# A seven-product matrix multiply: scaled fp16 and five products by quarters, against unscaled fp16 and six

## The chip, the cores and the metric

The kernel runs on one core of one Trainium2 chip. The metric is the device time of one execution in microseconds (us). Lower is better. Below, PE is the matrix engine, DVE the vector engine, ACT the scalar engine, POOL the GpSimd engine, and SP the engine whose queue issues every DMA here. SBUF is the on-chip memory of 128 partitions, PSUM the accumulators that matmuls write: eight banks of 128x512 float32.

## The reference

```python
B, S, D = 8, 2048, 2048
x = np.random.randn(B, S, D).astype(np.float32)
w = np.random.randn(D, D).astype(np.float32)

def reference(x, w):
    cs = np.cumsum(x, axis=1)
    diff = cs - (cs shifted by one row, first row zero)
    return np.matmul(diff, w).astype(np.float32)
```

The difference of a running sum is the input again, so what has to be computed is a product of a 16384x2048 matrix with a 2048x2048 matrix.

## The kernel before

**Tiles.** x is cut into 128 tiles of 128 rows. Tiles 0 to 3 are multiplied plainly while w is still arriving. The other 124 go in 31 groups of four tiles, called g, h = g+2, and their partners g+1 and h+1. One group is a block product: the left matrix has the quarters A11, A12 (tiles g and h, left and right half of the inner dimension) and A21, A22 (the partners), and w has the quarters B11, B12, B21, B22 of 1024x1024. Each group forms the result by Winograd's seven products instead of eight: P1 = A11 B11, P2 = A12 B21, P3 = S4 B22, P4 = A22 T4, P5 = S1 T1, S2 T2 and S3 T3. The sums S1 to S4 are made for every group, by DVE, from transposed x tiles in fp16. The sums T1 to T4 are made of w, once.

**Products and quarters.** A product taken whole costs 32 matmuls of 128x128 by 128x512 (line 532, `matmuls`). A product "by quarters" applies the same seven-product scheme once more inside itself, on quarters of 512: it costs 28 matmuls (line 554, `quarter`). It needs four sums of x pieces (128x512 fp16), and sums Q1 to Q4 of quarters of T or B (128x2048 fp16). In the class `Quarters` the seven steps are called slots:

```python
        def slot(self, i):
            h, g, b = self.h, self.g, self.right.b
            to, left, right, start = (
                (h[0], "a11", "t11", True),
                (h[1], "s1", "Q1", True),
                (h[0], "s2", "Q2", False),
                (g[0], "a12", "t21", False),
                (h[0], "s3", "Q3", False),
                (g[1], "s4", "t22", False),
                (h[0], "a22", "Q4", False),
            )[i]
            quarter(f"{self.name}.{i}", to, getattr(self, left), b[right], start)
            if i == 0:
                copy(f"{self.name}.first", g[0], h[0])
            elif i in (2, 4):
                copy(f"{self.name}.out{i}", self.lent, h[0])
```

The three copies are ACT's (line 571). With them go two DVE additions, `middle` and `last`, of a PSUM bank and a copy in SBUF (line 520). Sum s3 is POOL's, the other three are DVE's (line 520 too).

From the third group on, P1 to P5 go by quarters and S2 T2 and S3 T3 whole: 5 x 28 + 2 x 32 = 204 matmuls. The first group takes all seven whole (224), the second takes P2 and P3 by quarters (216).

Some Q sums stay in SBUF. Six are made anew in each group by DVE (`give`), into one buffer `flow` which every one of them shares. One more is brought back from DRAM (`bring`, 512 KB).

**Scaling.** x and w are scaled before the conversion to fp16: w by its largest magnitude (line 291, while it arrives, and line 415), each x tile by the mean of its absolute values. For a tile, ACT sums magnitudes (`weigh`, line 138), POOL and DVE make the scale and its reciprocal (lines 157, 159, 160), ACT converts (`narrow`, line 170), and two transposing DMAs bring the halves into the layout that PE needs (`turn`, line 186). Results are scaled back where they leave PSUM: `keep` copies a bank with a factor (ACT, line 568), and `add` adds a bank times a factor to what was kept (DVE, SCALAR_TENSOR_TENSOR, line 579). There are 20 of these additions in a group. Two finished results of a group go to DRAM for each pair of tiles, in 512 KB pieces (`put`).

**Order.** Every operation is recorded with a label. A table `places` written out by hand gives each label a position for the prelude, for single groups and (`None`) for all others; each engine issues its operations in that order and waits only by semaphores. So the engines' queues are fixed, and an operation that waits holds up all that stands behind it on its engine.

Of the kernel before, what the change touches and what calls it, by code (L numbers as in the profile page):

```python
# [10 lines left out]
def kernel(  # L11
# [17 lines left out]
    bf16 = mybir.dt.bfloat16  # L29
    f32 = mybir.dt.float32  # L30
    ADD = mybir.AluOpType.add
    SUB = mybir.AluOpType.subtract
    MUL = mybir.AluOpType.mult
    MAX = mybir.AluOpType.max
    AX = mybir.AxisListType
    COPY = mybir.ActivationFunctionType.Copy
    ABS = mybir.ActivationFunctionType.Abs
    TOP = 2048.0
    ROW = 4000.0
    TINY = 1e-34  # L40
# [4 lines left out]
    PERIOD = 2168  # L45
# [7 lines left out]
    W = [Wall[:, k, :] for k in range(KH)]  # L53
    whole = [t.rearrange("p (a h n) -> p a h n", a=2, h=2) for t in W]
    pieces = [
        t.bitcast(f16).rearrange("p (i n j c) -> p i j n c", i=4, j=2, c=NB) for t in W
    ]
    B11, T1, B12, T2, B21, T3, B22, T4 = (
        [p[:, i // 2, i % 2] for p in pieces] for i in range(8)
    )  # L60
    fours = Wall.bitcast(f16).rearrange("p k (i n j c) -> p k i j n c", i=4, j=2, c=NB)
    tiny = const.tile([P, 64], f32, name="tiny")
    sums_at = [tiny[:, ds(2 * i, 2)] for i in range(4)]
    means_at = [tiny[:, ds(i, 1)] for i in (8, 9, 13, 14)]
    uw, uinv, wred = (tiny[:, ds(10 + i, 1)] for i in range(3))
    scales_at = [tiny[:, ds(16 + i, 1)] for i in range(8)]
    units_at = [tiny[:, ds(24 + i, 1)] for i in range(8)]
    wmax = tiny[:, ds(32, 2 * KO)]
    waste = const.tile([P, NH], mybir.dt.uint8, name="waste")
    eye = waste[:, : 2 * P].bitcast(bf16)  # L70
    F = const.tile([P, 4, NH], f32, name="F")
    turned_x = [
        [const.tile([P, KH, P], f16, name=f"x{i}{j}") for j in range(2)] for i in range(4)
    ]

    arena = const.tile([P, 46 * 256], f32, name="arena")

    def area(kb, size, dtype):
        return arena[:, ds(kb * 256, size * 256)].bitcast(dtype) if dtype != f32 else arena[:, ds(kb * 256, size * 256)]

    ring = [area(2 * i, 2, bf16) for i in range(7)]
    results = [area(14 + 2 * i, 2, f32) for i in range(8)]
    xP = area(30, 16, bf16).rearrange("p (r k m) -> p r k m", r=PLAIN, k=KO)
    free = [area(4 * i, 4, f32).rearrange("p (n c) -> p n c", n=2) for i in (0, 1, 2, 4)]
    S1_at = area(12, 4, f16).rearrange("p (i n c) -> p i n c", i=2, n=2)
    rooms_at = area(20, 4, f16).rearrange("p (j c) -> p j c", c=NB)
    inner = area(24, 16, f16).rearrange("p (j c) -> p j c", c=NB)
    flow = area(40, 4, f16).rearrange("p (j c) -> p j c", c=NB)
    chain = area(44, 2, f32)
    psum = ctx.enter_context(tc.tile_pool(name="ps", bufs=1, space=bass.MemoryType.PSUM))  # L90
    banks = [psum.tile([P, NB], f32, name=f"b{i}") for i in range(8)]
    pairs = [banks[2 * i : 2 * i + 2] for i in range(4)]
# [11 lines left out]
    where = {}  # L104
    stage = [F[:, i, :] for i in range(4)]
    unit = {}
    sums_of = {}
    scales = {}

# [4 lines left out]
    def record(label, engine, ask):  # L114
        at = seen[period[0], label] = seen.get((period[0], label), 0) + 1
        if at > 1:
            label = f"{label}#{at}"
        ops.append((period[0], label, engine, ask))

# [3 lines left out]
    def load(t, i):  # L123
        if t < END:
            to = stage.pop(0)
            where.setdefault(t, [None, None])[i] = to
# [6 lines left out]
    def weigh_one(t, i):  # L133
        m, data = sums_of[t][:, i : i + 1], where[t][i]
        record(
            f"weigh{role(t)}.{i}",
            "act",
            lambda: nc.scalar.activation(waste, data, ABS, scale=1.0 / ROW, accum_out=m),  # L138
        )

    def weigh(t, sides=range(2)):
        if t < END:
            if t not in sums_of:
                sums_of[t] = sums_at[t % 4]
            for i in sides:
                weigh_one(t, i)

    def scale_of(t):
        if t < END:
            m2 = sums_of.pop(t)  # L150
            m = means_at[t % 4]
            s = scales[t] = scales_at[t % 8]
            u = unit[t] = units_at[t % 8]
            record(
                f"mean{role(t)}",
                "pool",
                lambda: nc.gpsimd.tensor_scalar(m, m2[:, :1], m2[:, 1:], TINY, ADD, MAX),  # L157
            )
            record(f"scale{role(t)}", "dve", lambda: nc.vector.reciprocal(s, m))  # L159
            record(f"unit{role(t)}", "pool", lambda: nc.gpsimd.tensor_scalar(u, m, uw, None, MUL))  # L160

    def narrowed(t):
        return where[t][0].bitcast(f16)

    def narrow_one(t, i):
        to, data, s = narrowed(t)[:, ds(i * NH, NH)], where[t][i], scales[t]
        record(
            f"narrow{role(t)}.{i}",
            "act",
            lambda: nc.scalar.activation(to, data, COPY, scale=s),  # L170
        )
        if i == 1 and t != PLAIN + 1:
            stage.append(where[t][1])

    def narrow(t, sides=range(2)):
        if t < END:
            for i in sides:
                narrow_one(t, i)

    turns_left = {}  # L180

    def place(t):
        return turned_x[(t - PLAIN) // 2 % 2 + 2 * (t % 2)]

    def turn_one(t, i):
        to, data = place(t)[i], narrowed(t)[:, ds(i * NH, NH)]
        record(f"turn{role(t)}.{i}", "sp", lambda: nc.sync.dma_start_transpose(to, data))
        turns_left[t] = turns_left.get(t, 2) - 1
        if turns_left[t] == 0 and t != PLAIN + 1:
            stage.append(where[t][0])  # L190

    def turn(t, halves=range(2)):
        if t < END:
            for i in halves:
                turn_one(t, i)

    def emit(places=None):
        def when(op):
            at, label = op[:2]
            own = places[at] if at in places else places[None]  # L200
            return at * PERIOD + own.get(label, 0)

        for _, _, engine, ask in sorted(ops, key=when) if places else ops:
            after(engine, ask)
        ops.clear()
# [9 lines left out]
    def eye_rows(i):  # L215
        own = ds(i, 32)
        record(
            "eye",
            "dve",
            lambda: nc.vector.tensor_scalar(  # L220
                eye[own, :],
                number[1][own, :],
                number[2][own, i : i + 1],
                None,
                mybir.AluOpType.is_equal,
            ),
        )
# [20 lines left out]
    def cast_x(q, a):  # L248
        to = resting(q, 0).bitcast(bf16).rearrange("p (a c) -> p a c", a=2)[:, a]
        src = resting(KH - 1 - q, a)  # L250
        record(f"cast x.{q}.{a}", "dve", lambda: nc.vector.tensor_copy(to, src))
        return to

    def turn_x(q, a, src, i):
        v = banks[i].bitcast(bf16)

        def some():
            for k in range(2 * KQ):
                at = ds(k * P, P)
                said = nc.tensor.transpose(v[:, at], src[:, at], eye)  # L260
# [11 lines left out]
    wb = {}  # L272
    rings = iter(ring * 6)

    def rest(h, ko):
        return whole[ko % KH][:, ko // KH, h, :]

# [6 lines left out]
    def taken(h, ko):  # L284
        src, most = rest(h, ko), wmax[:, ds(h * KO + ko, 1)]
        to = wb[h, ko] = next(rings)
        record(f"cast w.{h}.{ko}", "act", lambda: nc.scalar.copy(to, src))  # L287
        record(
            f"max w.{h}.{ko}",
            "dve",  # L290
            lambda: nc.vector.tensor_reduce(most, src, AX.X, MAX, apply_absolute_value=True),
        )
# [4 lines left out]
    def plain(h, r, ko):  # L297
        to, b = ps[r], wb[h, ko]

        def some():  # L300
            for n in here(h, r):
                said = nc.tensor.matmul(
                    to[n],
                    xP[:, r, ko, :],
                    b[:, ds(n * NB, NB)],
                    start=(ko == 0),
                    stop=(ko == KO - 1),
# [5 lines left out]
    results_at = iter(results * 2)  # L313

    def result(name, p, rows, columns, u=None):
        c = next(results_at)
        if u is None:
            record(f"{name}", "act", lambda: nc.scalar.copy(c, p))  # L318
        else:
            record(f"{name}", "act", lambda: nc.scalar.activation(c, p, COPY, scale=u))  # L320
        done.append(
            (f"put {name}", lambda: nc.sync.dma_start(out2[rows, columns], c))
        )
# [16 lines left out]

    for i in range(WARM):
        warm(i)
    AHEAD = 3
# [12 lines left out]
    for ko in range(KO - KQ):  # L356
# [20 lines left out]
    for ko in range(KO - KQ, KO):  # L377
        taken(0, ko)
    for ko in range(AHEAD):
        fetch(1, ko)  # L380
    for ko in range(AHEAD):
        taken(1, ko)
    for r in range(PLAIN):
# [1283 lines left out]
```

## Time and profile before

| | |
|---|---|
| runs, us | 1461.17, 1460.62, 1456.22 (median 1460.62) |
| span of the profiled execution, first to last instruction | 1457.7 us |
| PE busy | 1440.2 us, 99%, 6692 matmuls recorded |
| DVE busy | 1245.1 us, 85% |
| ACT busy | 1132.1 us, 78% |
| POOL busy | 288.1 us, 20% |
| DMA, 16 engines' share | 89.3% for the kernel's own queue |
| granted PE clock | 0.999 |

The profile gives no other time of the profiled execution than its span; the table's span lies between the fastest and the slowest run, and 2.9 us under the median. Busy shares are averages over the whole program: the prelude (some 90 us, in which w arrives), 31 groups, and the end. PE's busy time counts matmuls that overlap in its pipeline, so what a matmul costs is read from the distance of one group's matmuls to the next group's.

### The profile page before, as it was taken

The numbers are of one execution on the slowest core, as the hardware profiler recorded it, in microseconds if no ns is written. First come the engines' busy times: TensorE is split into PE (matmuls) and PEld (weight loads), VectorE is DVE, ScalarE is ACT, GpSimd is POOL, SyncE is SP. The second block draws the span as 40 slices with busy tenths as digits, with TensorE's granted clock in tenths as the row PEclk, the third lists the DMA queues.
The fourth block names the chain that finished last, engine by engine and source line by source line (L and its number), as shares of the span: only waits on it lengthen the run. The fifth ranks groups of instructions, "written<-read, shape, count | busy, mean of one in ns | idle before, by whom it ended". The sixth has DMA issues, their size and how long they took to land.

```text
span 1457.7 us, 20733 instructions
## 1 busy us (share of the span) xinstructions
PE 1440.2 (99%) x6692; PEld 652.4 (45%) x6698; DVE 1245.1 (85%) x2075; ACT 1132.1 (78%) x1742; POOL 288.1 (20%) x400
## 2 busy tenths in 40 slices
PE   8999999999999999999999999999999999999998
PEld 3444444444444444444444444444444444444443
DVE  6998898888888888889888889888888888898887
ACT  5886678877788877788877788877788777788773
POOL 0001122212222212222122122122122122122211
PEclk9999999999999999999999999999999999999999
DMA  9999879999888999889998889998899999889983
GB/s 354 359 255 274 220 222 250 261 263 249 252 242 241 262 266 243 239 248 243 273 269 238 236 249 240 272 258 248 223 263 247 266 253 260 224 247 260 263 212 135
DMA packets 348108, 367.33 MB, mean 252 GB/s; under 512 B 271456, under 2 KB 271456, under 8 KB 348000
## 3 DMA queue, kind: packets, MB, share of 16 engines
q1 hardware_dynamic: 348000, 366.02, 89.3%
q8 instruction: 52, 0.85, 0.2%
q14 instruction: 56, 0.46, 0.1%
HBM read 166.20 MB, written 134.74 MB: 206 GB/s over the span
## 4 chain that ended last, share of the span: by engine, by line
PE 92%; DMA 5%; ACT 1%; issue 1%; DVE 0%; SPq 0%; DVEq 0%; POOL 0%; ACTq 0%
PE b L554 60%; PE b L532 32%; DMA W<-in_w_dram 2%; DMA W<-in_x_dram 2%; DMA out_dram<-arena 0%; DMA x<-arena 0%; DMA F<-in_x_dram 0%; ACT waste L138 0%; ACT arena L287 0%; ACT F L170 0%; DVE arena L579 0%; ACT arena L318 0%; ACT arena L568 0%; ACT W L417 0%; SPq L245 0%
## 5 line engine op out<-in xcount | busy, mean ns | idle before, releaser
L532 PE MATMUL b<-W,x 128*128 128x512 f16 x2176 | 523.2, 379 | 0.6 <-DMA x<-F 0.6
L579 DVE SCALAR_TENSOR_TENSOR arena<-b,tiny,arena 128x512 f32<-128x512 f32 x612 | 439.7, 743 | 55.4 <-ACT arena L568 42.8
L554 PEld LDWEIGHTS <-arena 128*128 128x128 f16 x2700 | 264.0, 98 | 321.3 <-issue 3.5
L554 PE MATMUL b<-W,arena 128*128 128x512 f16 x1640 | 405.6, 379 | 0.6 <-ACT arena L571 0.6
L568 ACT ACTIVATE arena<-b,tiny 128x512 f32<-128x512 f32 x496 | 322.3, 685 | 51.4 <-PE b L532 39.4
L532 PEld LDWEIGHTS <-x 128*128 128x128 f16 x2176 | 212.9, 98 | 257.5 <-DMA x<-F 1.1
L170 ACT ACTIVATE F<-F,tiny 128x1024 f16<-128x1024 f32 x246 | 282.0, 1147 | 52.0 <-DVE tiny L159 47.0
L554 PE MATMUL b<-W,x 128*128 128x512 f16 x1180 | 297.1, 379 | 0.0
L571 ACT COPY arena<-b 128x512 f32<-128x512 f32 x294 | 169.7, 586 | 147.5 <-PE b L554 136.8
L138 ACT ACTIVATE waste<-F 128x1024 uint8<-128x1024 f32 x246 | 260.2, 1058 | 13.5 <-DMA F<-in_x_dram 11.7
L554 PE MATMUL b<-arena 128*128 128x512 f16 x1060 | 266.9, 379 | 0.5 <-DVE tiny L159 0.3
L520 POOL TENSOR_TENSOR arena<-x,x 128x512 f16<-128x512 f16 x118 | 142.7, 1210 | 543.9 <-PE b L554 511.9
L520 DVE TENSOR_TENSOR b<-b,arena 128x512 f32<-128x512 f32 x294 | 203.2, 692 | 38.1 <-ACT arena L571 37.3
L554 PEld LDWEIGHTS <-x 128*128 128x128 f16 x1416 | 138.5, 98 | 167.4 <-issue 0.7
L520 DVE TENSOR_TENSOR arena<-W 128x2048 f16<-128x2048 f16 (+1 forms) x127 | 149.4, 1177 | 2.8 <-PE b L554 2.5
L157 POOL TENSOR_SCALAR tiny<-tiny 128x1 f32<-128x1 f32 x124 | 41.8, 337 | 439.3 <-ACT waste L138 414.3
L571 ACT COPY b<-b 128x512 f32<-128x512 f32 x147 | 85.0, 578 | 35.8 <-DVE arena L579 20.6
L520 DVE TENSOR_TENSOR arena<-x,arena 128x512 f16<-128x512 f16 x118 | 50.2, 427 | 54.3 <-PE b L554 54.3
L520 DVE TENSOR_TENSOR x<-x,x 128x1024 f16<-128x1024 f16 x124 | 82.3, 681 | 0.2
L520 DVE TENSOR_TENSOR arena<-W,arena 128x2048 f16<-128x2048 f16 (+1 forms) x70 | 75.3, 1076 | 3.1 <-PE b L554 3.0
L160 POOL TENSOR_SCALAR tiny<-tiny 128x1 f32<-128x1 f32 x124 | 72.1, 583 | 0.7
L554 PE MATMUL b<-arena,x 128*128 128x512 f16 x236 | 60.2, 379 | 0.0
(46 smaller groups left out, 616.4 us busy)
## 6 DMA issues: line engine op xcount, KB each, us to landing
F<-in_x_dram SPq DMA_DIRECT2D x246, 512.0 KB, 5.5
out_dram<-arena SPq DMA_DIRECT2D x240, 512.0 KB, 5.4
W<-in_w_dram SPq DMA_DIRECT2D x32, 512.0 KB, 9.0
arena<-kept SPq DMA_DIRECT2D x29, 512.0 KB, 4.4
out_dram<-arena SPq DMA_DIRECT2D x32, 256.0 KB, 2.9
W<-in_x_dram SPq DMA_DIRECT2D x16, 256.0 KB, 7.6
x<-F SPq DMA_TRANSPOSE x246, 3.7
arena<-in_x_dram SPq DMA_DIRECT2D x2, 512.0 KB, 4.7
```

Source lines behind the costliest of these rows:

```text
L138: lambda: nc.scalar.activation(waste, data, ABS, scale=1.0 / ROW, accum_out=m),
L157: lambda: nc.gpsimd.tensor_scalar(m, m2[:, :1], m2[:, 1:], TINY, ADD, MAX),
L160: record(f"unit{role(t)}", "pool", lambda: nc.gpsimd.tensor_scalar(u, m, uw, None, MUL))
L170: lambda: nc.scalar.activation(to, data, COPY, scale=s),
L520: record(label, engine, lambda: on.tensor_tensor(dst, p, q, op))
L532: said = nc.tensor.matmul(to[n], a[k], b[k][:, n, :], start=(start and k == 0), stop=(k == KH - 1), skip_group_check=True,)
L554: said = nc.tensor.matmul(to, a[k], b[k], start=(start and k == 0), stop=(k == 3), skip_group_check=True)
L568: record(label, "act", lambda: nc.scalar.activation(c, p, COPY, scale=u))
L571: record(label, "act", lambda: nc.scalar.copy(to, p))
L579: label, "dve", lambda: nc.vector.scalar_tensor_tensor(c, p, u, c, MUL, ADD)
```

## The change

Nearly all of the kernel is written anew. What it does:

- **No scaling.** x and w are converted to fp16 as they are. `keep` and `add` lose their factors: additions become plain TENSOR_TENSOR instructions. `scale_of` (lines 157 to 160) goes. `weigh` stays, now behind `narrow`, and its sums are only kept. The maxima of w (line 291) and the scaling of w's blocks (line 415) go.
- **A guard and a general path.** At the end, DVE compares the kept sums with bounds (the sum of 1024 magnitudes of x between 256 and 2048 in each row, results of one group finite, one sum of w at least 4), POOL reduces the flags over partitions, and a register is loaded with the outcome. If it is 1, a loop over all 128 tiles computes everything again with scaling.
- **Six of seven products by quarters, in all 31 groups.** S3 T3 becomes P7, by quarters. S2 T2 stays whole and is called P6. A group has 6 x 28 + 32 = 200 matmuls.
- **Q sums.** Nothing goes to DRAM and back. Eleven Q sums are made in each group by DVE into `flow` (`ask`): Q1 and Q4 for P1, P2, P5, P3 and P4, and Q1 for P7.
- **Engines.** All four x sums of every product by quarters are DVE's. Additions of two buffers in SBUF, 128x512 float32, go to POOL, twelve in a group.
- **In-place sums.** S1 takes the place of A21, S2 of A11, S4 of A12, and S3 later the place of S1. The area for S1 goes.
- **Order.** Tiles of a group are now g, g+1, g+2, g+3; the order of the products is P1, P2, P5, P6, P3, then P4 and P7 side by side; all positions in `places` are new.

The core of the diff, cut:

```diff
-TOP = 2048.0
...
+    class Seven:
...
+        def slot(self, i):
+            n = self.name
+            if i == 0:
+                quarter(f"{n}.0", self.h0, self.a11, self.right.ask("t11"), True)
+                copy(f"{n}.first", self.g0, self.h0)
+            elif i == 1:
+                self.sum(1, self.r1, self.a21, self.a22, ADD)
+                self.sum(2, self.r2, self.r1, self.a11, SUB)
+                quarter(f"{n}.1", self.h1, self.r1, self.right.ask("Q1"), True)
+            elif i == 2:
+                quarter(f"{n}.2", self.h0, self.r2, self.right.ask("Q2"), False)
+                copy(f"{n}.out2", self.lent, self.h0)
+                tensor(f"{n}.middle", self.g1, self.h1, self.lent, ADD)
+            elif i == 3:
+                quarter(f"{n}.3", self.g0, self.a12, self.right.ask("t21"), False)
+            elif i == 4:
+                self.sum(3, self.r1, self.a11, self.a21, SUB)
+                quarter(f"{n}.4", self.h0, self.r1, self.right.ask("Q3"), False)
+                copy(f"{n}.out4", self.lent, self.h0)
+            elif i == 5:
+                self.sum(4, self.r2, self.a12, self.r2, SUB)
+                quarter(f"{n}.5", self.g1, self.r2, self.right.ask("t22"), False)
+            elif i == 6:
+                quarter(f"{n}.6", self.h0, self.a22, self.right.ask("Q4"), False)
+
+    def plus(label, c, p, engine="dve"):
+        tensor(label, c, c, p, ADD, engine)
...
+        plus("P1.last", P1.h1, lx)
...
+        for c, p, n in ((C11g, zv[0], "g"), (C11h, zv[1], "h")):
+            for i in range(2):
+                plus(f"C11{n}+P2.{i}", c[:, i, :], p[i])
+        plus("P2.last", C11h[:, 1, :], lz, "pool")
...
+        for t, s in ((g, "g"), (h, "h")):
+            tensor(f"S1{s}", flat(t + 2, 0), flat(t + 2, 0), flat(t + 2, 1), ADD)
+            tensor(f"S2{s}", flat(t, 0), flat(t + 2, 0), flat(t, 0), SUB)
+            tensor(f"S4{s}", flat(t, 1), flat(t, 1), flat(t, 0), SUB)
...
+        for u, v, p, s, t in ((C21g, C22g, zv[0], "g", g), (C21h, C22h, zv[1], "h", h)):
+            c = free.pop(0)
+            for i in range(2):
+                tensor(f"C12{s}.{i}", c[:, i, :], p[i], v[:, i, :], ADD)
+                if s == "h" and i == 1:
+                    plus("P3.last", c[:, i, :], lz, "pool")
+                plus(f"C12{s}+C21.{i}", c[:, i, :], u[:, i, :], "pool")
...
+        for c, v, p, s in ((C21g, C22g, xy[0], "g"), (C21h, C22h, xy[1], "h")):
+            for i in range(2):
+                plus(f"C21{s}+P7.{i}", c[:, i, :], p[i])
+                if s == "h" and i == 1:
+                    plus("P7.last", c[:, i, :], lx, "pool")
+                plus(f"C22{s}+C21.{i}", v[:, i, :], c[:, i, :], "pool")
...
+        plus("P4.last", C21h[:, 1, :], lz, "pool")
...
+    v = nc.values_load(fault[0:1, 0:1], min_val=0, max_val=1)
+    with tc.If(v > 0):
...
+        with tc.For_i(0, M // P, 1) as i:
```

More of the change, by code (lines that the diff above doesn't have):

```diff
@@ L74 @@
     ]
-    arena = const.tile([P, 46 * 256], f32, name="arena")
+    arena = const.tile([P, (4 * 5 + 24) * 256], f32, name="arena")
     def area(kb, size, dtype):
[L79 to L89, printed above, removed]
+        some = arena[:, ds(kb * 256, size * 256)]
+        return some.bitcast(dtype) if dtype != f32 else some
+    at = 4 * 5
+    pair_at = [area(4 * i, 4, f32).rearrange("p (n c) -> p n c", n=2) for i in range(5)]
@@ L131, in load, with narrowed @@
             )
[L133 to L141, printed above, removed]
[L142 to L148 removed]
+    def narrowed(t, i):
+        return where[t, i].bitcast(f16)[:, :NH]
@@ L192, in turn @@
[L192 to L205, printed above, removed]
+                f"weigh{role(t)}.{i}",
+                "act",
```

1127 lines of the change are left out of this document (380 added, 747 removed), and 953 rows, old and new, of the table places.

## The prediction

> **What bounds the kernel now.** I read the page first, then the chain that ended last, then the windows, then single engines over one group.
>
> ```profile
> span 1457.7 us, 20733 instructions
> PE 1440.2 (99%) x6692; PEld 652.4 (45%) x6698; DVE 1245.1 (85%) x2075; ACT 1132.1 (78%) x1742; POOL 288.1 (20%) x400
> PE 92%; DMA 5%; ACT 1%; issue 1%; DVE 0%; SPq 0%; DVEq 0%; POOL 0%; ACTq 0%
> ```
>
> The last row is the share of the chain by engine. PE holds 92% of it, so the number of matmuls sets the time, as long as nobody else becomes later than PE.
>
> ```profile
> 702.33 12.95 PE b L554 x60
> 746.37 12.95 PE b L554 x60
> 0.00:90.00 90.00, 80.33 (x400) 37.05 (x406) 71.53 (x95) 69.00 (x85) 3.64 (x13) 1.00 0.97 331
> 702.33:746.37 44.04, 44.04 (x205) 19.95 (x204) 37.61 (x64) 35.26 (x55) 9.31 (x13) 1.00 0.88 257
> ```
>
> The first two rows are the same piece of the chain in two groups: they lie 44.04 us apart, and a group has 204 matmuls, so one costs 44.04/204 = 0.2159 us. The last two rows are windows, with the columns PE, PEld, DVE, ACT, POOL, granted clock, DMA share, GB/s. In one group PE is busy for 44.04 of 44.04 us, at full clock. DVE stands still for 6.4 us, and PE feels none of that.
>
> **Matmuls.** Before there are 224 + 216 + 29 x 204 = 6356 in the groups, after it 31 x 200 = 6200. The prelude's stay. 156 x 0.2159 = 33.7 us go, and a group could take 200 x 0.2159 = 43.2 us.
>
> **DVE.** This is where the change can fail, so I price each kind by the distance from its start to the start of the next instruction. DVE's instructions overlap a little, so that their own durations say too much.
>
> ```profile
> 703.80 0.41 DVE L520 TENSOR_TENSOR arena<-x,arena 128x512 f16<-128x512 f16 x1
> 704.13 0.69 DVE L520 TENSOR_TENSOR b<-b,arena 128x512 f32<-128x512 f32 x1
> 708.19 0.69 DVE L520 TENSOR_TENSOR b<-b,arena 128x512 f32<-128x512 f32 x1
> 708.79 0.68 DVE L520 TENSOR_TENSOR arena<-x,x 128x1024 f16<-128x1024 f16 x1
> 712.33 0.68 DVE L520 TENSOR_TENSOR x<-x,x 128x1024 f16<-128x1024 f16 x1
> 712.93 1.22 DVE L520 TENSOR_TENSOR arena<-W 128x2048 f16<-128x2048 f16 x1
> 714.06 0.68 DVE L520 TENSOR_TENSOR x<-arena,x 128x1024 f16<-128x1024 f16 x1
> 714.66 0.74 DVE L579 SCALAR_TENSOR_TENSOR arena<-b,tiny,arena 128x512 f32<-128x512 f32 x1
> 715.33 0.15 DVE L159 RECIPROCAL tiny<-tiny 128x1 f32<-128x1 f32 x1
> 715.40 0.73 DVE L579 SCALAR_TENSOR_TENSOR arena<-b,tiny,arena 128x512 f32<-128x512 f32 x1
> ```
>
> Starts subtracted: 0.33 us for a quarter sum (128x512 fp16), 0.60 for an addition with a PSUM operand, 0.60 for a half sum (128x1024), 1.13 for a Q sum (128x2048), 0.67 for a scaled addition, 0.07 for a reciprocal. The group before is then 20 x 0.67 + 10 x 0.60 + 6 x 1.13 + 15 x 0.33 + 8 x 0.60 + 4 x 0.07 = 36.2 us, and the window says 37.61. So 1.4 us a group go to dependent neighbours and the like.
>
> After, for each group: 24 quarter sums (7.9 us), 11 Q sums (12.4), 8 half sums (4.8), and 24 float32 additions with a PSUM operand (6 `middle`, `P1.last`, `keep C22h.1`, 16 additions of results: 14.4). Together 39.5 us, with the same 1.4 us 40.9. That is under 43.2, with 2.3 us left of the former 6.4.
>
> **POOL, and what it does to DVE.** POOL's twelve additions are 128x512 float32 from SBUF to SBUF, which the trace does not show. The nearest row is its fp16 sum of the same shape, 1.16 us: 12 x 1.16 = 13.9 us of 43.2, so POOL itself has room. But it gets in DVE's way:
>
> ```profile
> 174.97 1.16 POOL L520 TENSOR_TENSOR arena<-x,x 128x512 f16<-128x512 f16 x1 [4.92 <-PE b L554]
> 175.03 1.63 DVE L520 TENSOR_TENSOR arena<-x,x 128x1024 f16<-128x1024 f16 x1
> 199.23 1.15 POOL L520 TENSOR_TENSOR arena<-x,x 128x512 f16<-128x512 f16 x1 [6.52 <-PE b L554]
> 199.30 2.16 DVE L520 TENSOR_TENSOR arena<-W 128x2048 f16<-128x2048 f16 x1
> 242.80 2.19 POOL L520 TENSOR_TENSOR arena<-x,x 128x512 f16<-128x512 f16 x1 [3.20 <-PE b L554]
> 243.89 1.38 DVE L520 TENSOR_TENSOR arena<-x 128x512 f16<-128x512 f16 x1
> 727.45 1.16 POOL L520 TENSOR_TENSOR arena<-x,x 128x512 f16<-128x512 f16 x1 [4.07 <-PE b L554]
> 727.61 0.74 DVE L579 SCALAR_TENSOR_TENSOR arena<-b,tiny,arena 128x512 f32<-128x512 f32 x1
> 728.27 0.62 DVE L520 TENSOR_TENSOR arena<-arena,x 128x512 f16<-128x512 f16 x1
> ```
>
> A DVE sum of two SBUF operands that meets a POOL sum is late: 1.63 instead of 0.68, 2.16 instead of 1.22, 1.38 instead of 0.41, 0.62 instead of 0.41. That is 0.95, 0.94, 0.97 and 0.21 us. The scaled addition at 727.61, with a PSUM operand, keeps its 0.74. [...]
>
> What this costs after the change is the unknown. The steady group before has five such POOL sums and pays 0.21 us: 0.04 each, because four of them run beside additions with a PSUM operand or beside an idle DVE. At that rate, and with two-SBUF work at 25.1 of 43.2 us instead of 16.5 of 44.04, twelve cost 12 x 0.04 x 1.55 = 0.7 us. At the other end, 43 of DVE's 67 instructions have two SBUF operands: 0.64 x the mean of the four collisions, 0.77 us, is 0.49 us each, 5.9 us a group. I take 0.7, since the steady row is from a static order with the same pattern in each group, and the large collisions are all from the first groups. DVE then stands at 41.6 of 43.2 us. With 1.6 us of slack in place of 6.4, some waits that were hidden will show; I allow 0.3 us a group, a fifth of that slack: 31 x 0.3 = 9.3 us.
>
> **ACT and DMA.**
>
> ```profile
> L571 ACT COPY arena<-b 128x512 f32<-128x512 f32 x294 | 169.7, 586 | 147.5 <-PE b L554 136.8 <-DVE b L520 4.0 <-DMA out_dram<-arena 1.0
> L287 ACT CAST arena<-W 128x1024 bf16<-128x1024 f32 x32 | 32.4, 1053 | 16.6 <-DMA W<-in_w_dram 15.0 <-PE b L302 1.5
> L138 ACT ACTIVATE waste<-F 128x1024 uint8<-128x1024 f32 x246 | 260.2, 1058 | 13.5 <-DMA F<-in_x_dram 11.7
> ```
>
> ACT gets 29 copies out of PSUM (17.0 us), 8 conversions (8.4) and 8 weighings (8.5): 33.9 us, against 35.26 in the window. Loads, transposes and stores stay, 8 each in a group, and the 512 KB from DRAM go; at a DMA share of 0.88 that is room, though not much. I cost both at nothing; PE is the cover.
>
> **Prelude.**
>
> ```profile
> L291 DVE TENSOR_REDUCE tiny<-W 128x1 f32<-128x1024 f32 x32 | 37.3, 1212 | 4.3 <-DMA W<-in_w_dram 4.0
> ```
>
> In the first 90 us PE ran 314 full matmuls (67.8 us) and 86 short ones (some 12), so 10 us are lost there to arriving data. DVE sheds 37.3 us of maxima and must now prepare all seven products for the first group: 24 differences at 0.60 and 17 wide sums at 1.13, 33.6 us. About even; 0, from -10 to +10.
>
> **End.**
>
> ```profile
> 1451.01 2.73 DVE L579 SCALAR_TENSOR_TENSOR arena<-b,tiny,arena 128x512 f32<-128x512 f32 x4 [0.48 <-ACT arena L568]
> out_dram<-arena SPq DMA_DIRECT2D x32, 256.0 KB, 2.9
> L406 POOL PARTITION_ALL_REDUCE tiny<-tiny x1 | 0.4, 382 | 59.8 <-DVE tiny L402 59.8
> ```
>
> Now the last addition ends at 1453.74, its store lands 2.9 us later, and the program ends 1.1 us after that. Added are `P4.last` on POOL (1.16), the reduction (0.38) and a comparison, then a word read into registers and a jump over the general path, which no row shows. It runs beside the last store: 0 if the read and the jump are short, two transfers of 2.9 us if each of them waits for one, 5.8. I take 3.
>
> **Sum.** 1457.7 - 33.7 + 9.3 + 0 + 3 = 1436.3 us as a span; the median of the runs lies 2.9 us above the profiled span, so 1439 us.
>
> **Rival 1: DVE becomes the pace, through POOL.** An exclusion that costs c for each POOL sum makes a DVE group of 40.9 + 12c. Below c = 0.19 PE hides it. Beyond, each 0.1 us is 1.2 us a group and 37 us in all. Without any loss in the groups the time is 1430 us (1457.7 - 33.7 + 3 + 2.9); the gain is used up where 31 groups lose 31 us, 1.0 us each, at c = 0.27. At 0.49 it is 46.8 us a group, 1430 + 31 x 3.6 = 1542 us, far slower. For it: 2.3 us of slack against twelve sums that start as soon as a DVE addition releases them, while DVE has already gone on to its next sum. Against it: 24 PSUM additions, 14.4 us, beside which 13.9 us of POOL work can lie. A middle value, c = 0.34, gives 45.0 us and 1486. [...]
>
> **Rival 2: x comes late.**
>
> ```profile
> x<-F SPq DMA_TRANSPOSE x246, 3.7
> ```
>
> P7 reads S3, which sits in the place of the partners' left halves, to the end of the group, so their transposes (turn6, turn7) now wait for the last products. S1 of the next group needs both halves, 68 matmuls (14.7 us) after the group's first. Narrowing is done by then, and four transposes of 3.7 us one behind another are 14.8 us: just enough. If S1 waits, every DVE instruction behind it waits, `P2.s4` and `P2.middle` first, and PE with them. A quarter of a transpose exposed (0.9 us a group) gives 1430 + 28 = 1458, no change; a whole one 1545. It decides from 0.7 us a group on.
>
> **Rival 3: the guard fires** and the loop runs: 128 x 64 matmuls, 1769 us more at least, over 3200. A sum of 1024 magnitudes of normal numbers is about 817, inside 256 to 2048. Chance 0.01.
>
> **How the numbers follow.** PE keeps the pace: 0.56 (1422 to 1453). Rival 1, slower: 0.29 (1468 to 1542). Rival 2 or a small c, near no change: 0.14. Rival 3: 0.01. Within 0.5% (7.3 us, about what a measurement of this kernel tells from no change) are 1453 to 1468. So faster 0.56, same 0.14, slower 0.30. The range runs from 1422 (period 43.2, prelude 8 us better) to 1490, a little above rival 1's middle value; what is left out is its upper half, rival 3, and little below. The forecast's own range is 1422 to 1453.
>
> **What would show it.** Right: groups 43.2 to 43.5 us apart, DVE busy 40 to 42 us a group, POOL about 14, few DVE sums stretched; the end within 9 us of the last matmul. Wrong by rival 1: DVE busy for nearly all of a longer group, many fp16 sums at twice their time beside POOL, PE idle before `quarter` released by DVE. By rival 2: DVE idle before a half sum released by a transposing DMA. A POOL addition much longer than 1.16 us would make rival 1 out of my forecast at once.

## The result, and the profile after

The changed kernel takes 1665.45 us (median of 4 runs, 1663.08 to 1666.97), the kernel before in the same runs 1460.89 us. The ratio is 1.140, with a 95% interval of 1.138 to 1.142. The forecast was 1439 us, somewhat faster, with a range up to 1490. It is wrong in sign. Rival 1, DVE as the pace through POOL, is what happened, and above its upper end of 1542 us.

The page of the changed kernel, its first lines:

```profile
span 1663.1 us, 20749 instructions
PE 1491.3 (90%) x6542; PEld 632.5 (38%) x6542; DVE 1551.0 (93%) x2144; ACT 1042.5 (63%) x1716; POOL 599.1 (36%) x377
```

PE has 150 recorded matmuls fewer (156 were planned) and is busy for 90% of the span only. DVE went from 85% to 93%. One stretch of 90 us in the middle of the program, first of the kernel before, then of the changed one (columns as in the prediction's windows: PE, PEld, DVE, ACT, POOL, granted clock, DMA share, GB/s):

```profile
800.00:890.00 90.00, 90.00 (x419) 40.78 (x418) 77.14 (x129) 72.40 (x114) 18.61 (x26) 1.00 0.90 251
```
```profile
800.00:890.00 90.00, 83.42 (x365) 35.34 (x364) 86.73 (x122) 56.99 (x97) 33.73 (x21) 0.98 0.78 210
```

PE starts 365 matmuls where it started 419, and DVE works for 86.73 of 90 us: 96%. DMA, ACT and PE all became less busy and POOL, at 33.73, is far from full, so DVE is what is left. The distance from one group's first matmul to the next group's is 50.8 us (median of the groups), where it was 44.04 and was to be 43.2 to 43.5.

The groups of instructions, DVE's sums and POOL's (of POOL's the waits are shown too):

```profile
L115 POOL TENSOR_TENSOR arena<-arena 128x512 f32<-128x512 f32 x372 | 598.6, 1623 | 1053.7 <-DVE arena L115 729.2 <-ACT arena L118 131.2 <-ACT b L118 123.6
L115 DVE TENSOR_TENSOR arena<-W 128x2048 f16<-128x2048 f16 x344 | 491.5, 1429 | 15.2 <-PE b L429 14.5
L115 DVE TENSOR_TENSOR x<-x,x 128x1024 f16<-128x1024 f16 x248 | 193.4, 791 | 1.0
L115 DVE TENSOR_TENSOR arena<-x 128x512 f16<-128x512 f16 x186 | 140.7, 767 | 1.0
L115 DVE TENSOR_TENSOR arena<-x,x 128x512 f16<-128x512 f16 x186 | 130.6, 702 | 6.2 <-PE b L429 5.9
L115 DVE TENSOR_TENSOR arena<-arena,b 128x512 f32<-128x512 f32 x372 | 244.2, 676 | 11.5 <-PE b L429 10.6 <-POOL arena L115 0.3 <-ACT F L153 0.3
```

A quarter sum of 128x512 fp16, 0.41 us in the prediction's rows, takes 0.767 or 0.702 us on average in the two kinds shown; the other two kinds take 0.575 (`arena<-x,arena`) and 0.436 (`arena<-arena,x`), so not all of them meet POOL alike. A Q sum takes 1.429 instead of 1.22. The additions with an operand in PSUM (`arena<-arena,b`) keep their 0.68. And most of POOL's idle time is ended by a DVE instruction.

Single instructions show how that comes about. DVE and POOL in one stretch of a group (start, duration):

```profile
531.12 8.75 POOL L115 TENSOR_TENSOR arena<-arena 128x512 f32<-128x512 f32 x6 [1.95 <-ACT b L118]
533.62 0.69 DVE L115 TENSOR_TENSOR b<-b,arena 128x512 f32<-128x512 f32 x1
534.23 1.27 DVE L115 TENSOR_TENSOR arena<-arena,b 128x512 f32<-128x512 f32 x2
535.42 1.92 DVE L115 TENSOR_TENSOR arena<-W 128x2048 f16<-128x2048 f16 x1
537.26 1.48 DVE L115 TENSOR_TENSOR arena<-x,arena 128x512 f16<-128x512 f16 x1
538.67 1.48 DVE L115 TENSOR_TENSOR arena<-x 128x512 f16<-128x512 f16 x1
540.83 1.39 POOL L115 TENSOR_TENSOR arena<-arena 128x512 f32<-128x512 f32 x1 [0.96 <-DVE arena L115]
541.01 2.29 DVE L115 TENSOR_TENSOR arena<-W 128x2048 f16<-128x2048 f16 x1
```

Six POOL sums run from 531.12 to 539.87. Three DVE additions with PSUM operands beside them take their usual time, 0.69 for one and 1.27 for two. The three sums from SBUF that follow take 1.92, 1.48 and 1.48 us, each about 0.7 to 1.1 us too much. At 541.01 a Q sum that begins 0.18 us after a POOL sum takes 2.29 us, 1.07 too much: about what is then left of the POOL sum.

Counted over the whole trace, 307 of DVE's sums of two SBUF operands begin while a POOL sum runs, when 0.96 us of it is left on average. Of these, 295 are longer than they are without POOL (experiment 1), by 0.86 us on average. Of the 1067 others none is longer by more than 0.02 us, not even those during which a POOL sum begins. Nor is one of the 191 additions with a PSUM operand that begin beside a POOL sum longer by more than 0.03 us. So DVE pays where it comes second, and that happens 295 times for 372 POOL sums. The other way round, the 253 POOL sums that begin while a DVE sum from SBUF runs take 1.79 us on average, the 119 others 1.26 to 1.31.

### The profile page after: what moved, and what is told of

It reads as the page before. It is cut to its first block, busy times and chain, and to the rows that moved or that the text cites. A ratio compares the mean times of both kernels' runs of the same rounds, so it can differ in the third digit from the quotient of the medians.

```text
span 1663.1 us, 20749 instructions
## 1 busy us (share of the span) xinstructions
PE 1491.3 (90%) x6542; PEld 632.5 (38%) x6542; DVE 1551.0 (93%) x2144; ACT 1042.5 (63%) x1716; POOL 599.1 (36%) x377
## 5 line engine op out<-in xcount | busy, mean ns | idle before, releaser
L115 POOL TENSOR_TENSOR arena<-arena 128x512 f32<-128x512 f32 x372 | 598.6, 1623 | 1053.7 <-DVE arena L115 729.2
L118 ACT COPY arena<-b 128x512 f32<-128x512 f32 x729 | 406.1, 588 | 367.9 <-PE b L429 197.0
L115 DVE TENSOR_TENSOR arena<-W 128x2048 f16<-128x2048 f16 x344 | 491.5, 1429 | 15.2 <-PE b L429 14.5
L429 PE MATMUL b<-W,x 128*128 128x512 f16 x1488 | 389.0, 389 | 7.6 <-DMA out_dram<-arena 4.3
L153 ACT ACTIVATE F<-F 128x1024 f16<-128x1024 f16 x248 | 262.1, 1058 | 0.0
L118 ACT CAST F<-F 128x1024 f16<-128x1024 f32 x248 | 254.5, 1051 | 3.5 <-DMA F<-in_x_dram 3.5
L115 DVE TENSOR_TENSOR arena<-arena,b 128x512 f32<-128x512 f32 x372 | 244.2, 676 | 11.5 <-PE b L429 10.6
L518 PE MATMUL b<-W,x 128*128 128x512 f16 x992 | 248.7, 379 | 0.4 <-DVE x L115 0.4
L429 PE MATMUL b<-arena,x 128*128 128x512 f16 x744 | 190.8, 379 | 13.0 <-DVE arena L115 5.0
L115 DVE TENSOR_TENSOR arena<-x 128x512 f16<-128x512 f16 x186 | 140.7, 767 | 1.0
L115 DVE TENSOR_TENSOR arena<-x,x 128x512 f16<-128x512 f16 x186 | 130.6, 702 | 6.2 <-PE b L429 5.9
```

Source lines behind the costliest of these rows:

```text
L115: record(label, engine, lambda: on.tensor_tensor(dst, p, q, op))
L118: record(label, "act", lambda: nc.scalar.copy(to, p))
L153: lambda: nc.scalar.activation(other, data, ABS, accum_out=m),
L429: said = nc.tensor.matmul(to, a[:, ds(k * P, P)], b[:, k, :], start=(start and k == 0), stop=(k == 3), skip_group_check=True,)
L518: said = nc.tensor.matmul(to[n], half(t, 0)[:, k, :], T2[k][:, n, :], start=False, stop=(k == KH - 1), skip_group_check=True,)
```

## The experiments

The theory: POOL's twelve float32 sums from SBUF and DVE's sums of two SBUF operands exclude each other, and DVE has become the pace. Its rivals: DVE is too slow through its own work (the in-place sums, eleven Q sums); the new order or the transposes are late; the guard costs much. Experiments 1 to 4 ran beside each other (the kernel before: 1460.2 us), then 5 and 7 (1460.2), then 6, 8 and 9 (1460.5). All but 7 start from the changed kernel; 7 starts from the kernel before.

**1. No POOL sums.**

```diff
     def plus(label, c, p, engine="dve"):
+        if engine == "pool":
+            return
         tensor(label, c, c, p, ADD, engine)
```

> The twelve POOL additions of a group are left out (their terms are missing from the result); all else, order included, stays. Theory 1, POOL and DVE exclude each other: DVE falls from 50.5 us a group to 39.5 + 1.4 = 40.9, PE becomes the pace at 43.2 to 43.8 us a group, and the time is 1663 - 31 x 7 = 1446 us (1435 to 1460). Rival A, the new order makes DVE, ACT and PE wait for each other whatever POOL does: groups stay above 48 us, over 1585 us. Rival B, DVE's own list was summed too low: the group stays at DVE's true sum, 45 us or more, over 1490 us, with no DVE instruction stretched.

Measured: 1455.33 us, ratio 0.996 [0.9946, 0.9974]. That is 210 us less, a little more than the whole loss of 204.6. Page line, window and two groups of this kernel:

```profile
PE 1424.4 (98%) x6542; PEld 635.6 (44%) x6542; DVE 1305.1 (90%) x2144; ACT 1040.7 (72%) x1716; POOL 0.5 (0%) x5
```
```profile
800.00:890.00 90.00, 89.83 (x414) 40.07 (x413) 83.89 (x139) 65.18 (x109) 0.00 (x0) 1.00 0.89 239
```
```profile
L115 DVE TENSOR_TENSOR arena<-W 128x2048 f16<-128x2048 f16 x344 | 418.8, 1218 | 24.0 <-PE b L429 20.8
L115 DVE TENSOR_TENSOR arena<-x 128x512 f16<-128x512 f16 x186 | 75.4, 417 | 1.1 <-PE b L429 0.2
```

DVE runs the same 2144 instructions in 1305.1 us instead of 1551.0. So 372 POOL sums cost DVE 245.9 us, 0.66 us each. By kinds, the Q sums give back 72.7 us and the quarter sums `arena<-x` 65.3 (767 to 417 ns). Groups are 43.73 us apart. The loss goes with the POOL sums; in-place sums, order and transposes alone bring no such loss.

**2. The same sums on DVE.**

```diff
-        tensor(label, c, c, p, ADD, engine)
+        tensor(label, c, c, p, ADD, "dve")
```

> The twelve POOL additions are done by DVE, at their places in the order; POOL is empty. Theory 1: DVE's group is 40.9 + 12 x 0.60 to 0.65 = 48.1 to 48.7 us, less than the 50.5 with POOL's help, so 1663 - 31 x 2.1 = 1598 us (1580 to 1612). Rival A: the order is what costs, and 7.2 to 7.8 us more on the engine that is already late make the group longer, 50.5 + 7.5, some 1890 us. Rival B: likewise longer than with POOL's help.

Measured: 1701.46 us, ratio 1.165 [1.163, 1.168]: neither of the two values. DVE's work is as worked out, and the sums of two SBUF operands are at their own length again:

```profile
PE 1492.2 (88%) x6542; PEld 635.3 (37%) x6542; DVE 1527.3 (90%) x2516; ACT 1047.9 (62%) x1716; POOL 0.5 (0%) x5
L115 DVE TENSOR_TENSOR arena<-W 128x2048 f16<-128x2048 f16 x344 | 418.5, 1216 | 17.8 <-PE b L429 17.6
```

1527.3 - 1305.1 = 222.2 us for 372 sums: 0.60 us each. On POOL the same sum costs DVE 0.66. POOL takes nothing off DVE here. What was missed is the idle time. DVE is busy for 94% of three stretches of 90 us, that is 48.6 us a group, but groups are 51.9 us apart. The waits of PE and of DVE in this kernel (total us, times, longest):

```profile
PE b L429 <- ACT arena L118: 63.4, 49, 2.4
PE b L429 <- ACT b L118: 55.2, 52, 2.8
PE b L429 <- DVE arena L115: 51.7, 78, 4.0
```
```profile
DVE arena L115 <- PE b L429: 44.9, 71, 1.5
DVE arena L115 <- DMA out_dram<-arena: 31.8, 32, 3.6
DVE b L115 <- ACT arena L118: 20.7, 28, 1.7
```

PE waits for ACT's copies and for DVE's sums; DVE waits for PE, for a store and for ACT's copies. In this kernel, with its fixed queues tied to each other, the busiest engine doesn't run without gaps.

**3. POOL writes, but reads nothing.** POOL's sums become instructions that write zeros into the same buffers, at the same places of the order; the sums themselves are left out.

```diff
+        if engine == "pool":
+            record(label, "pool", lambda: nc.gpsimd.memset(c, 0.0))
+        else:
             tensor(label, c, c, p, ADD, engine)
```

> Each of POOL's twelve additions is replaced by a memset of the same 128x512 float32 buffer: the same queue, the same waits and writes, but nothing read (those results are zero). [...] If any POOL instruction that writes excludes too, DVE's sums are stretched by up to a memset each: 0.5 to 1.2 us x 0.68/1.27 x 12, 3 to 8 us a group, 1500 to 1640 us. Rival A: over 1585 us.

Measured: 1455.82 us, ratio 0.997 [0.996, 0.9985], as without POOL (1455.33); a stretch by writes was expected to give 1500 us or more.

```profile
L481 POOL MEMSET arena<- 128x512 f32 x372 | 185.7, 526 | 1260.1 <-DVE arena L115 1244.3 <-ACT b L118 14.0
L115 DVE TENSOR_TENSOR arena<-x 128x512 f16<-128x512 f16 x186 | 75.5, 417 | 1.0
```

POOL works 186 us at the same places of its queue, and DVE's quarter sums take 417 ns as without it. Nor is it that the writes are too short to meet DVE: 83 of DVE's sums from SBUF begin while one of them runs, and none is longer by more than 0.02 us. So neither POOL's places in the order nor its writes into SBUF are the cause. What is left is that the sums read, or the kind of instruction, which is another here too.

**4. No guard.** The comparison of sums, the read of the register and the general path are left out.

```diff
-    judge()
...
-    v = nc.values_load(fault[0:1, 0:1], min_val=0, max_val=1)
-    with tc.If(v > 0):
...
```

> The comparisons, the reduction over partitions, the register and the general path are left out; the sums that they judge are still made. The profile after shows the last matmul's start 12.6 us before the end, against 5.9 us before, with 6.2 us in which POOL waits for nothing that is shown ahead of the reduction. If the guard's chain is the tail: 1665 - 7 to 9 = 1657 us. If the last stores are the tail anyway: no change within 1 us.

Measured: 1658.09 us, ratio 1.135 [1.133, 1.137]. The guard costs 7.4 us in all; the time from the start of the last matmul to the end goes from 12.6 to 6.4 us, and groups stay where they were. The end of the changed kernel shows what it is:

```profile
1651.54 0.69 DVE L115 TENSOR_TENSOR arena<-arena,b 128x512 f32<-128x512 f32 x1 [0.33 <-POOL arena L115]
1659.18 0.37 POOL L694 PARTITION_ALL_REDUCE tiny<-tiny  x1 [6.45 <-issue]
1659.58 0.21 DVE L700 TENSOR_SCALAR tiny<-tiny 128x1 int32<-128x1 f32 x1 [7.36 <-POOL tiny L694]
```

POOL stands still for 6.45 us ahead of the reduction with nothing that it waits for. That the reduction is the first of its kind on POOL isn't enough for the stop. In experiment 3, where POOL has only written before, the same reduction, also the first there, starts 0.13 us after the last write:

```profile
1445.70 0.53 POOL L481 MEMSET arena<- 128x512 f32 x1 [2.42 <-DVE arena L115]
1446.36 0.35 POOL L697 PARTITION_ALL_REDUCE tiny<-tiny  x1
```

Behind the multiplications of experiment 6 the stop is 7.60 us. So it matters what POOL ran before; what fills the stop isn't shown. The read and the jump are in the 3.3 us from 1659.79 to the end at 1663.1.

**5. Which of the twelve sums.** One kernel keeps only the four sums called `last` on POOL and leaves out the eight result sums; the other the opposite.

```diff
+        if engine == "pool" and "last" not in label:
+            return
```

> Of POOL's twelve additions a group, the eight of results (C12+C21, C22+C21) are left out and the four named last stay. Theory 1, at the 0.66 us for each sum that DVE's stretched instructions show ((1551.0 - 1305.1) us of DVE time over 372 sums): DVE is busy 40.75 + 4 x 0.66 = 43.4 us, just under the 43.73 us of a group without POOL sums, so the time is 1456 to 1470 us. If the cost were not by sum but by the order as a whole, it would lie in the middle, near 1525 us.

> The other way round: the four named last are left out, the eight of results stay. Theory 1: DVE is busy 40.75 + 8 x 0.66 = 46.0 us, beyond PE, and idle 0 to 2 us as in the kernel after: 46.0 to 48.0 us a group, 1455 + 31 x (2.3 to 4.3) = 1526 to 1588 us. A cost in proportion to the sums left, with no threshold: 1455 + 210 x 8/12 = 1595 us.

Measured: 1513.96 us, 1.037 [1.034, 1.040], for the four; 1554.36 us, 1.064 [1.061, 1.067], for the eight. Page lines and windows of the first and of the second:

```profile
PE 1445.6 (96%) x6542; PEld 630.3 (42%) x6542; DVE 1378.8 (91%) x2144; ACT 1042.6 (69%) x1716; POOL 227.0 (15%) x129
```
```profile
800.00:890.00 90.00, 87.35 (x395) 37.98 (x394) 85.66 (x133) 62.71 (x105) 15.69 (x8) 1.00 0.88 232
```
```profile
PE 1448.6 (93%) x6542; PEld 630.5 (41%) x6542; DVE 1452.4 (94%) x2144; ACT 1042.2 (67%) x1716; POOL 384.9 (25%) x253
```
```profile
800.00:890.00 90.00, 85.21 (x386) 36.99 (x385) 87.54 (x130) 61.09 (x102) 25.10 (x16) 1.00 0.83 228
```

Both kinds of sums stretch DVE alike: (1378.8 - 1305.1)/124 = 0.59 us each for the four, (1452.4 - 1305.1)/248 = 0.59 for the eight, somewhat less than the 0.66 with all twelve. The eight came out inside what was expected. The four did not: 1514 us is nearer to the 1525 of the other value, a cost of the order as a whole. But DVE's own rows show the cost by sum; what comes on top is idle time, and this is the second thing learned. DVE is busy for 43.4 us of a group, about what PE needs, and yet the groups are 45.7 us apart. PE's waits in this kernel, and POOL's row:

```profile
PE b L429 <- ACT b L118: 19.6, 51, 0.5
PE b L429 <- DVE arena L115: 16.9, 30, 2.1
```
```profile
L115 POOL TENSOR_TENSOR arena<-arena 128x512 f32<-128x512 f32 x124 | 226.5, 1826 | 1274.7 <-DVE arena L115 600.4 <-ACT b L118 224.3 <-DMA F<-in_x_dram 213.2
```

PE stands 36.5 us in all before products, waiting for ACT's copies and DVE's sums, while DVE still has some 2.3 us of idle time in each group. The added work did not go into these gaps: 2.4 us more of it on DVE made the groups 2.0 us longer.

**6. One operand.** POOL's sum becomes a multiplication by 1 that reads one operand; the sums are left out.

```diff
-        tensor(label, c, c, p, ADD, engine)
+        if engine == "pool":
+            record(label, "pool", lambda: nc.gpsimd.tensor_scalar(c, c, 1.0, None, MUL))
+        else:
+            tensor(label, c, c, p, ADD, engine)
```

> Each of POOL's twelve additions is replaced by a multiplication of the same buffer by 1.0 in place: one operand read instead of two (the added terms are missing from the result). Theory 1, reading from SBUF is what excludes, for as long as the instruction lasts: DVE's sums of two SBUF operands are stretched by at most one such instruction's time; if it takes 0.6 us, about 0.3 us each, DVE is busy 44.5 us a group and the time is 1490 to 1560 us. If only POOL instructions with two read operands exclude: no stretch, 1455 us, as with the memsets.

Measured: 1497.7 us, ratio 1.026 [1.023, 1.029], inside the range of the first value.

```profile
L481 POOL TENSOR_SCALAR arena<-arena 128x512 f32<-128x512 f32 x372 | 688.3, 1868 | 795.7 <-DVE arena L115 779.2 <-ACT b L118 13.2 <-DMA out_dram<-arena 1.0
L115 DVE TENSOR_TENSOR arena<-x 128x512 f16<-128x512 f16 x186 | 96.9, 532 | 1.0
```

Quarter sums go from 417 to 532 ns on average, and DVE's total from 1305.1 to 1371.6 us, 0.18 us an instruction. An instruction of POOL that reads one operand is enough for the effect on quarter sums; the sum with two costs nearly four times as much, 0.66. And this one doesn't hold DVE up for all of its length. It takes 1.87 us on average, longer than the sum, but of the 590 DVE sums from SBUF that begin while one runs only 197 are longer, none by more than 0.47 us. Here a Q sum keeps its 1.22 us in the middle of seven of them:

```profile
530.75 11.94 POOL L481 TENSOR_SCALAR arena<-arena 128x512 f32<-128x512 f32 x7 [3.42 <-DVE arena L115]
535.10 1.22 DVE L115 TENSOR_TENSOR arena<-W 128x2048 f16<-128x2048 f16 x1
```

As it is another instruction too, the number of operands isn't parted here from the kind.

**7. The kernel before with more POOL work.** Eighty more sums of 128x128 float32 on POOL in each group, in a buffer of their own; in a second kernel, writes of zeros instead.

```diff
+        for i in range(80):
+            record(
+                f"extra.{i}",
+                "pool",
+                lambda: nc.gpsimd.tensor_tensor(extra, extra, extra, ADD),
+            )
```

> The kernel before, with 80 POOL sums of a 128x128 float32 buffer of their own added to each group from the second on; nobody reads them. Theory 1: at 0.3 to 0.4 us each they are 24 to 32 us of POOL work a group. The kernel after shows 7.9 us of stretched DVE for 15.2 us of POOL sums; with two-SBUF sums at 16.5 of 44.04 us here, against 25.1 of 43.73, that is 0.34 us for each us of POOL, 8 to 11 us a group, against 6.4 us of DVE's idle time: 2 to 5 us a group, 1460 + 30 x (2 to 5) = 1520 to 1610 us. If exclusion isn't what made the kernel after slow: within 1% of before.

> As the one with 80 more POOL sums, but with 80 memsets of the same buffer, which read nothing: the control for POOL's queue, behind which the scales of x wait. Theory 1: within 1% of before, 1446 to 1475 us, and no DVE sum stretched more than before. If POOL's queue alone delays the scales: as slow as with the sums.

Measured: 1795.37 us, ratio 1.230 [1.226, 1.233], and 1478.99 us, 1.013 [1.010, 1.016]. Windows of the two:

```profile
800.00:890.00 90.00, 73.88 (x319) 31.24 (x317) 67.33 (x102) 58.68 (x93) 79.81 (x148) 0.96 0.64 181
```
```profile
800.00:890.00 90.00, 89.29 (x411) 39.89 (x410) 78.46 (x129) 70.57 (x111) 51.08 (x186) 1.00 0.89 248
```

The dose was too large: both came out above what was expected. With the sums POOL itself is busy for 79.81 of 90 us and DVE for only 67.33, so POOL's own queue, in which s3 and the scales of x stand behind the extra sums, is the pace. The times say little, therefore, about the exclusion in the kernel before.

The single instructions say more. With the extra sums, 733 of DVE's sums from SBUF begin while one of them runs, and 550 are longer, by up to 0.26 us. With the extra writes 385 begin so, and none is longer by more than 0.02 us. That is the exclusion, and its control, in the kernel before.

One thing was not expected: with the writes, DVE's sums are stretched more than before all the same, by the five POOL sums that were always there. These keep their places in POOL's order, and DVE's order is unchanged, but POOL reaches them at other times. In each steady group they now hold up three DVE sums, by 0.21, 0.55 and 0.98 us, where they held up one by 0.20. One of the new meetings:

```profile
807.95 1.16 POOL L524 TENSOR_TENSOR arena<-x,x 128x512 f16<-128x512 f16 x1 [0.61 <-PE b L558]
807.99 1.67 DVE L524 TENSOR_TENSOR arena<-x,x 128x1024 f16<-128x1024 f16 x1
```

**8. Without Q sums.** Experiment 1's kernel, and the eleven Q sums left out from the second group on, to see what PE alone needs.

```diff
+            if period[0] == 0:
                 tensor(f"{self.name}.{name}", flow, self.s[p], self.s[q], op)
```

> As the kernel without POOL sums, and from the second group on the eleven Q sums of a group are left out too (the matmuls read what the buffer last held): DVE has 12.4 us less, 28 us a group. Open is why a group without POOL sums takes 43.73 us where 200 matmuls at 0.2159 are 43.18. If short waits for DVE and ACT in the tight order are the reason: 43.2 us, 1455 - 30 x 0.5 = 1438 to 1442 us. If it is PE's own (more semaphores, shorter runs of matmuls): 43.7 us stays, 1453 to 1456 us.

Measured: 1447.97 us, ratio 0.992 [0.989, 0.995], between the two values expected. Groups are 43.48 us apart; DVE is busy for 59.43 of 90 us. Of the 0.55 us by which experiment 1's groups are longer than 200 matmuls at 0.2159, DVE's load accounts for about half. The traces show where the rest is. In sixteen groups in the middle of each, matmuls start 0.216 us apart, except at a few fixed places of the group. Here there are three: before the group's 121st and 173rd matmul PE waits for a DVE addition into a bank (0.16 and 0.07 us), before the 169th for a copy of ACT's (0.09 us). Experiment 1's groups have the same three and a fourth, 0.25 us for a DVE sum in SBUF before the 97th. So both parts are short waits for DVE and ACT, and none is PE's own.

**9. Another order.** C12g.0, C12g.1, C12h.1 and S3h in a row on DVE, so that POOL's sums begin beside additions with a PSUM operand.

```diff
+            run = ("C12g.0", "C12g.1", "C12h.1", "S3h")
+            if label in run and at < 30:
+                return at * PERIOD + max(own[one] for one in run[:2]) + 0.1 * run.index(label)
```

> The kernel after, with one change of order: DVE does C12g.0, C12g.1 and C12h.1 in a row and S3h behind them, so that the POOL sums which they release can run beside additions with a PSUM operand. If the order sets how often POOL and DVE meet: one or two of the twelve sums no longer stretch a DVE sum, 0.6 to 1.3 us a group, 1625 to 1650 us. If the meetings are only moved to the next sums: within 10 us of 1665.

Measured: 1757.55 us, ratio 1.204 [1.201, 1.208], with one run of 3600.2 us. The edit changes more than an order: C12h.1 now writes a result buffer whose former content is not stored yet, so the computation differs too. As a test of order it is inconclusive; the DVE sums held up by POOL did not become fewer (298, against 295). In the run of 3600.2 us the time agrees with the general path running: 1843 us more, beside the 1769 at least that the prediction gave it.

## Why the prediction was wrong

**The step that failed** is the price c of a POOL sum to DVE. It was taken as 0.06 us (0.7 us a group); it measured 0.66 us, 7.9 a group. Both factors of that price were too small: the prediction took one meeting for five POOL sums, at 0.21 us, and the trace has 295 for 372, four for five, at 0.86 us. DVE's group is then 40.75 (experiment 1) + 7.9 = 48.6 us, and with 2 us that it can't fill 50.6: the mean distance of the groups is 50.6.

The prediction had seen the exclusion, and chose between the two ends of c by the wrong row. The steady group before has five POOL sums and one collision, of 0.21 us. That was scaled up, because the group's order is fixed; but it is the order that the change rewrites, and five sums in one group are no rate. It owed its 0.21 us to luck in the times at which POOL came: in experiment 7 writes that hold up nothing were enough to turn it into 1.74 us a group, with the same five sums, and the order of the old instructions on each engine unchanged. The four collisions themselves, 0.77 us on average, stood in the rows, and 0.66 is nearest to them. The end of 0.49 us was no bound either, since it multiplied that mean by a share of meetings (the largest stretch in the changed kernel is 1.11 us, beside POOL sums of 1.26 and more); and its share of 0.64 was below the measured 0.79. Nor are the large collisions all from the first groups, as the prediction says for its choice: from 1277 us on, in the last groups, whose order is another too, there are four more, of 0.58 to 1.01 us. One is this sum, 0.41 us long when it meets nothing:

```profile
1300.43 1.15 POOL L520 TENSOR_TENSOR arena<-x,x 128x512 f16<-128x512 f16 x1 [4.94 <-DVE arena L520]
1300.44 1.43 DVE L520 TENSOR_TENSOR arena<-arena,x 128x512 f16<-128x512 f16 x1
```

What the prediction said for rival 1, that a POOL sum released by DVE starts when DVE has gone on to its next sum, is seen in the trace: a DVE instruction ends 729.2 of POOL's 1053.7 us of idle time. It isn't shown to be why c is so large, for the four `last` sums alone (experiment 5), where DVE ends 600.4 of 1274.7 us, cost nearly as much each.

**The slack** was the second error. By the prediction 2.3 us of DVE's idle time were there to be used and any c below 0.19 was hidden. Experiment 5 (four sums, 2.4 us a group) shows that they weren't: groups 45.7 us apart at 43.4 us of DVE work. At its own c, rival 1's formula of 40.9 + 12c gives 48.8 us; the 2 us above that are this.

**What meets what** was read rightly from the four collisions in the prediction's rows. The three DVE additions with a PSUM operand beside the six POOL sums keep their time, 0.69 us for one and 1.27 for two, and the three sums from SBUF behind them are 0.7 to 1.1 us longer. Beside POOL's writes DVE's quarter sums keep their 417 ns (experiment 3). A POOL sum holds a DVE sum up nearly to its own end: in 306 of the 307 meetings the time added is at most 0.13 us less than what is left of the POOL sum. The multiplication of experiment 6 doesn't: 393 of the 590 DVE sums that begin during one keep their time. The amount, 0.66 us a sum, is the runs'.

**Smaller terms.** A float32 POOL sum was taken as 1.16 us; the fastest here take 1.26 to 1.27, and with waits 1.62 on average. The waits in a group paced by PE were allowed 0.3 us and measured 0.55 (experiment 1). The prelude, taken at 0 and from -10 to +10, measured 10.0 us more to the first group (its first matmul is at 84.0, before at 74.0), the upper end; and the first group itself is 4.8 us longer than the others in experiment 1 (48.6). The end was taken as 3 us and measured 6.5 (the last matmul starts 12.6 us before the end, before 6.1), most of it POOL's stop of 6.45; all that follows DVE's comparison, the read and the jump among it, fits into 3.3 us.

**What held.** The matmuls and their price: PE needs 43.2 us a group (200 matmuls at 0.2159; a matmul's own record before is 379 ns long on average, so the records overlap), and experiment 1's groups are 43.73 apart. DVE's own work: 40.9 us forecast, 40.75 measured without POOL. ACT and DMA are no bound (in the changed kernel's 90 us ACT is busy for 56.99, and the DMA share is 0.78). Rival 2 didn't come: DVE's waits have no transposing DMA among them. Rival 3 didn't come in the changed kernel.

**What the change could have brought.** With all twelve sums left out it is 1455.33 us, 0.4% under before. Of the 33.7 us of matmuls removed, 10.0 went to the prelude and 2.1 to the end. The groups took another 17.4: from the first matmul of the groups to the last, experiment 1's kernel loses 22.84 us against 0.2159 a matmul, and the kernel before 5.48. That leaves 4.2 us; 4.1 were measured between the profiled spans and 4.9 between the medians. No version here that computes all of the result beats the kernel before: on POOL, where they are now, and on DVE the sums cost alike.

**Open.** How much of the 7.9 us an order could save that puts POOL's sums beside DVE's 14.4 us of additions with a PSUM operand; no clean test of this was made. Why a POOL multiplication with one operand holds up some of the DVE sums that begin beside it and not others. What makes POOL stand still for 6.45 us ahead of the reduction.

## What to carry to other kernels

Before a sum from SBUF goes from a full vector engine to GpSimd, price it by the time that it takes from the vector engine: here 0.66 us, against 0.60 for doing the sum on the vector engine itself. Price it by the collisions themselves and not by how rare they are in an order that the change rewrites: a change of POOL's times alone made them cost eight times as much here. The idle time of an engine with a fixed queue wasn't slack here: 1 to 3 us of it per group stayed, however full the queue was. And the quick proof is to leave the suspect out, then to replace it by an instruction that writes in the same place and reads nothing.

## What was not expected of the hardware

None of the 83 DVE sums that began beside a POOL write of 128x512 float32 (526 ns) was longer by more than 0.02 us; a POOL multiplication that reads one operand cost DVE 0.18 us, a sum that reads two 0.66. The POOL reduction over partitions behind such sums started 6.45 us late, with no wait behind it (6.4 and 6.8 us in the two kernels of experiment 5); behind writes of zeros it started 0.13 us after them.
